# First loads of the attention stage and of the chain issued from ScalarE's queue, in a hybrid attention and RWKV-7 layer

## Chip, cores and metric

The kernel runs on one core of a Trainium2 chip. The metric is the device time of one execution in microseconds. The profile is of one execution of its own.

## What is computed

One layer over 2048 latent tokens of width 1024, arranged as a grid of 32 rows by 64 columns, with a prefix of 256 context tokens. A modulated input goes through one projection. Its columns feed eight heads of neighbourhood attention and eight RWKV-7 heads that run over the tokens in both directions. Both results go through an output projection, a layer norm and a squared-ReLU MLP.

```
p = modulate(x, sh1, sc1) @ w_in ; pc = modulate(xc, sh1c, sc1c) @ w_in
y_na = neighbourhood_attention(q, k, v, kc, vc, na_rpb)   # 8 x 16 window and all 256 context keys
...
S = S * w_t - s_kk (kk_t * a_t) + v_t k_t ; y_t = S r_t    # RWKV-7, two directions, from a state made by the context
...
x = layer_norm(ALPHA * x + g1 * concat(y_na, y_rw) @ w_out)
x = layer_norm(ALPHA * x + g2 * squared_relu_mlp(modulate(x, sh2, sc2)))
```

## The kernel before

The program has four stages. The first projects all tokens and writes queries, keys, values and the RWKV terms to scratch tensors in DRAM (`Q`, `KR` rotated keys, `KC` context keys, `VN` values, `AR`, `BK`, `VT`, `XB` for the chain). The second, `tail`, runs the attention and the RWKV chain side by side until about 1790 us; then come the output tiles with the rest of the chain, and two stages of the MLP.

The attention works on four pairs of heads. For a pair, 32 tiles of 128 queries are handled in groups of four. `front` makes scores of one tile against the window (`psl`, from the keys `kr` and the queries `qz`) and against the context (`psx`, from `kc`), takes the softmax on VectorE and ScalarE; `back`, three tiles later, transposes and multiplies with the values `vw` and `vc`. All products are made from a high and a low part of each operand: a load brings the 32-bit value, ScalarE casts the high part, VectorE (later GpSimd) subtracts it for the low part.

The chain goes in 36 steps of 64 tokens, both directions per step. `chain_pre` loads a step's `bkc`, `ks`, `SV` and `xz` and makes its first products; `chain_main` does the state update. In `tail` the two are woven: the first tile of the attention, then `chain_pre` for step 0, the second tile, then each step with the tiles that fall to it. The values of the first pair, `vload(0, 0, 8)`, are put after the chain's first `xz` load.

The order on each engine is not the order of the code alone: the framework schedules the instructions, and each engine and each DMA queue then runs its own in order. All loads before the change go through SyncE's queue (`nc.sync`). A DMA is issued by an engine as an instruction, which first waits for its semaphores. There are eight completion semaphores, `DMAHW0` to `DMAHW7`, handed out in turn over the DMAs of both queues; a DMA waits until the DMA that had the same semaphore before it has landed.

The names and lines of the opening, in the numbering of the kernel before: `kload` L916 and L917, L918 (keys of the first pair in two parts of 768 and 1280 columns), `pair` L937 (`bu`), L943 and L944 (`kc` and its cast), L947 (`vc`), `queries` L958, L960 and L961 (`qz`, casts, low parts; four DMAs of 64 KB per group), `vload` L925 (16 DMAs of 128 KB), `chain_pre` L1118 (`bkc`), L1125 (`ks`), L1128 (`SV`, four DMAs of 64 KB), L1130 (`xz`), the stores of rotated keys of the stage before, L717 (`KR<-rot`), and the last projected rows, L453.

Of the kernel before, what the change touches and what calls it, by code (L numbers as in the profile page):

```python
# [17 lines left out]
L = 256  # L18
# [10 lines left out]
CW = (0, 8, 24, 32)  # L29
# [28 lines left out]
def f32(ap):  # L58
    return ap.bitcast(F32)


class Kern:
# [858 lines left out]
    def vload(self, p, b0, b1):  # L921
        v = self.VN[L:, p * 128:(p + 1) * 128].rearrange("(b r x) c -> r x b c", r=4, x=64)
        for c in range(4):
            for r in range(4):
                self.nc.sync.dma_start(self.vw[r * 32:r * 32 + 32, b0:b1, c, :], v[r, CW[c]:CW[c] + 32, b0:b1, :])  # L925

    def attention(self):

        nc, a = self.nc, self.a
# [4 lines left out]
        def pair(p):  # L934
            E = nc.gpsimd if p else nc.vector
            u = self.at2.tile([128, 3, 12, 32], F32, name="bu")
            nc.sync.dma_start(u, a["rpb"][p])  # L937
            m = self.at2.tile([128, 3, 12, 32], F32, name="bm")
            for k in range(3):
                E.tensor_tensor(u[:, k], u[:, k], self.cmask[:, k, None, :].to_broadcast([128, 12, 32]), ALU.add)  # L940
                E.tensor_tensor(m[:, k], u[:, k], self.rmask[:, :, None].to_broadcast([128, 12, 32]), ALU.add)
            kc = [self.at2.tile([128, L], F32R, name="kc%d" % j) for j in range(2)]
            nc.sync.dma_start(f32(kc[1]), self.KC[p])  # L943
            nc.scalar.copy(kc[0], f32(kc[1]))  # L944
            E.tensor_tensor(kc[1], f32(kc[1]), f32(kc[0]), ALU.subtract)
            vc = self.at2.tile([128, 2, 128], F32, name="vc")
            nc.sync.dma_start(vc, self.VN[0:L, p * 128:(p + 1) * 128].rearrange("(m q) c -> q m c", q=128))  # L947
            return u, m, kc, vc

        def queries(g):  # L950

            p, hf, c, _ = tiles[g * 4]
            z = self.qz[g % 2]
            h, l = z
            for d in range(2):
                hs = slice(d * 64, d * 64 + 64)
                for j in range(2):
                    nc.sync.dma_start(f32(l[hs, j, :, hs]), self.Q[p, hs, j].rearrange("k (a c x) -> k c a x", c=4, x=64)[:, c, hf * 4:hf * 4 + 4, :])  # L958
            for j in range(2):
                nc.scalar.copy(h[:, j], f32(l[:, j]))  # L960
                (nc.gpsimd if g > 1 else nc.vector).tensor_tensor(l[:, j], f32(l[:, j]), f32(h[:, j]), ALU.subtract)  # L961

        def blocks(q):

            return {0: (1, 3), 7: (0, 2)}.get(q, (0, 3))

        def front(n):
            p, hf, c, i = tiles[n]
            q = hf * 4 + i
            if n == 0:  # L970
                self.kload(0, 0, 12)
                self.kload(0, 12, 32)
                st["pair", 0] = pair(0)
            if n == 0:
                queries(0)
            if i == 0 and n < 124:
                queries(n // 4 + 1)
            u, bm, kc, vc = st["pair", p]
            qh, ql = self.qz[n // 4 % 2]
            k0, k1 = blocks(q)  # L980
            w = (k1 - k0) * 128
            psl = self.psA.tile([128, 512], F32, name="psl")
            r = 4 * (q - 1 + k0)
            kh, kl = [x[:, r:r + 4 * (k1 - k0), CW[c]:CW[c] + 32] for x in self.kr]
            for j, (x, y) in enumerate(((qh, kh), (ql, kh), (qh, kl))):
                nc.tensor.matmul(psl[:, :w], lhsT=x[:, 0, i, :], rhs=y, start=j == 0, stop=j == 2)
            psc = self.psA.tile([128, 256], F32, name="psx")
            for j, (x, y) in enumerate(((qh, kc[0]), (ql, kc[0]), (qh, kc[1]))):
                nc.tensor.matmul(psc, lhsT=x[:, 1, i, :], rhs=y, start=j == 0, stop=j == 2)
            S = self.at2.tile([128, 640], F32, name="S", bufs=4)  # L990
            m = self.at2.tile([128, 8], F32, name="mx", bufs=4)

            lo, co = (k0 * 128, 384) if hf == 0 else (256, 0)
            sl, sc = S[:, lo:lo + w], S[:, co:co + 256]
            bias = (bm if k1 - k0 == 3 else u)[:, CK[c], 4 if q == 0 else 0:8 if q == 7 else 12, :]
            nc.vector.tensor_tensor_reduce(sl, psl[:, :w], bias.rearrange("p a b -> p (a b)"), 1.0, -3.0e38, ALU.add, ALU.max, m[:, 0:1])
            nc.vector.tensor_reduce(m[:, 1:2], psc, AX.X, ALU.max)
            nc.vector.tensor_scalar(m[:, 2:3], m[:, 0:1], m[:, 1:2], -1.0, ALU.max, ALU.mult)
            nc.scalar.activation(sc, psc, AF.Exp, bias=m[:, 2:3], accum_out=m[:, 4:5])
            nc.scalar.activation(sl, sl, AF.Exp, bias=m[:, 2:3], accum_out=m[:, 3:4])  # L1000
            nc.vector.tensor_tensor(m[:, 5:6], m[:, 3:4], m[:, 4:5], ALU.add)
            nc.vector.reciprocal(m[:, 6:7], m[:, 5:6])
            x = S[:, min(lo, co):min(lo, co) + w + 256]
            nc.gpsimd.tensor_scalar(x, x, m[:, 6:7], 1.0, ALU.mult, ALU.mult)
            st["S", n] = S, min(lo, co), w + 256
            if i == 3 and c == 3 and p < 3:
                if hf == 0:
                    self.kload(p + 1, 0, 12)
                else:
                    self.kload(p + 1, 12, 32)  # L1010
                    st["pair", p + 1] = pair(p + 1)
# [66 lines left out]
        for n in range(ASTEPS):  # L1078
            if n < 128:
                front(n)  # L1080
            if 0 <= n - LAG < 128:
                back(n - LAG)
            if n - LAG >= 128:
                for f in pieces[:5]:
                    f()
                del pieces[:5]
            if n == 1:
                with self.tc.issue_after(self.xzd):
                    self.vload(0, 0, 8)
            yield  # L1090
# [9 lines left out]
    def chain_pre(self, s, order):  # L1100

        nc = self.nc
        c = [order[d][s] for d in range(2)]
        last = s == 35
        T2 = lambda n, sh: self.ch2.tile(sh, F32, name=n)
        hs = [slice(0, 64), slice(64, 128)]
# [3 lines left out]
        sv = T2("SV", [128, 2, 4, 2, 64])  # L1110
# [14 lines left out]
                    nc.sync.dma_start(ks[h][hs[h], d, :, 0:w], self.AR[hs[h], d, c[d], :, 0:w])  # L1125
        for h in range(2):
            for d in range(2):
                nc.sync.dma_start(sv[hs[1 - h], d, :, h, :],  # L1128
                                  self.VT[c[d] * 64:(c[d] + 1) * 64, :].rearrange("t (p h v) -> t p h v", p=4, h=2)[:, :, h, :])
        self.xzd = nc.sync.dma_start(xz, self.XB.rearrange("s d (c p) t -> s (d c) p t", p=4)[:, two]).ins  # L1130
        ab = T2("ab", [128, 2, 4, 64])
# [802 lines left out]
```

## Time and profile before

| | us |
|---|---|
| median of 3 runs | 3431.05 (3422.89 to 3433.24) |
| profiled execution, its time | 3430.26 |
| its span, first to last instruction | 3428.5 |
| TensorE busy | 3193.7 (93%) |
| VectorE busy | 2603.2 (76%) |
| ScalarE busy | 1523.1 (44%) |
| GpSimd busy | 511.6 (15%) |
| last product of the projections | 1002.4 |
| first product of the attention | 1017.2 |
| last scores of the attention | 1731 |

The span is cut into stretches by the starts of the instructions. SyncE's and ScalarE's DMA instructions are in the timeline of these engines, with the time that the issue took; the transfer comes after it. A wait is put down to the instruction that came last.

### The profile page before, as it was taken

The numbers are of one execution on the slowest core, as the hardware profiler recorded it, in microseconds if no ns is written. First come the engines' busy times: TensorE is split into PE (matmuls) and PEld (weight loads), VectorE is DVE, ScalarE is ACT, GpSimd is POOL, SyncE is SP. The second block draws the span as 40 slices with busy tenths as digits, with TensorE's granted clock in tenths as the row PEclk, the third lists the DMA queues.
The fourth block names the chain that finished last, engine by engine and source line by source line (L and its number), as shares of the span: only waits on it lengthen the run. The fifth ranks groups of instructions, "written<-read, shape, count | busy, mean of one in ns | idle before, by whom it ended". The sixth has DMA issues, their size and how long they took to land. (4 is left out here: it accounts for less than half of the span.)

```text
span 3428.5 us, 65249 instructions
## 1 busy us (share of the span) xinstructions
PE 3193.7 (93%) x25176; PEld 2605.3 (76%) x25176; DVE 2603.2 (76%) x4907; ACT 1523.1 (44%) x2891; POOL 511.6 (15%) x535
## 2 busy tenths in 40 slices
PE   7999899899978999989879988999999989999998
PEld 3888888789866777767657766777788868888886
DVE  5567977888687778767768877767767657899878
ACT  4555465456535445454442123343433343337333
POOL 0000000000005454544343322000000000010001
PEclk9999999999989999999989988999999999999999
DMA  7487376726666655554374546665644455545441
GB/s 242 134 246 209 95 178 161 223 76 168 169 191 156 140 133 129 138 131 117 98 202 147 172 155 217 213 205 186 215 155 137 154 193 162 167 153 210 148 155 73
DMA packets 765338, 561.67 MB, mean 164 GB/s; under 512 B 380412, under 2 KB 653564, under 8 KB 763620
## 3 DMA queue, kind: packets, MB, share of 16 engines
q1 hardware_dynamic: 691738, 523.14, 51.8%
q10 hardware_dynamic: 73290, 34.37, 3.5%
q8 instruction: 198, 3.24, 0.4%
q14 instruction: 112, 0.92, 0.1%
HBM read 359.70 MB, written 197.66 MB: 163 GB/s over the span
## 5 line engine op out<-in xcount | busy, mean ns | idle before, releaser
L450 PE MATMUL psm<-xh,wh 128*128 128x386 f32 (+1 forms) x1104 | 381.7, 348 | 16.5 <-ACT row L453 9.9
L450 PE MATMUL psm<-xl,wh 128*128 128x386 f32 (+1 forms) x1104 | 381.4, 346 | 2.7 <-DVE xl L421 2.6
L450 PE MATMUL psm<-xh,wl 128*128 128x386 f32 (+1 forms) x1104 | 377.0, 341 | 0.0
L450 PEld LDWEIGHTS psm<-xh,wh 128*128 128x128 f32 x1104 | 210.9, 192 | 42.7 <-ACT row L453 18.7
L450 PEld LDWEIGHTS psm<-xl,wh 128*128 128x128 f32 x1104 | 210.7, 191 | 17.8 <-issue 7.3
L450 PEld LDWEIGHTS psm<-xh,wl 128*128 128x128 f32 x1104 | 210.6, 191 | 4.9 <-issue 3.7
L1531 PE MATMUL psa<-xh,w1h 128*128 128x512 f32 x512 | 204.3, 399 | 4.0 <-DVE p L1557 3.7
L1795 POOL TENSOR_TENSOR acc<-acc,g 128x1024 f32<-128x1024 f32 x8 | 28.9, 3641 | 1186.9 <-DVE acc L1738 1186.9
L1531 PE MATMUL psa<-xl,w1h 128*128 128x512 f32 x512 | 202.7, 396 | 0.0
L1531 PE MATMUL psa<-xh,w1l 128*128 128x512 f32 x512 | 201.8, 395 | 0.0
L1679 ACT CAST ah<-al 128x1024 fp32r<-128x1024 f32 x98 | 103.0, 1051 | 216.5 <-DMA al<-HU 204.8
L760 DVE TENSOR_TENSOR stmp<-mp,xp 128x1 f32<-128x1 f32 (+30 forms) x310 | 179.2, 578 | 18.3 <-POOL xp L752 6.8
L1680 DVE TENSOR_TENSOR al<-al,ah 128x1024 fp32r<-128x1024 f32 x98 | 121.3, 1237 | 86.8 <-ACT ah L1679 86.7
L436 DVE TENSOR_TENSOR wl<-wst,wh 128x1024 fp32r<-128x1024 f32 x81 | 98.7, 1219 | 92.0 <-ACT wh L435 69.6
L1462 ACT CAST w1h<-w1s 128x512 fp32r<-128x512 f32 x96 | 59.6, 621 | 238.3 <-DVE w1s L1451 84.5
L1729 PE MATMUL psqb<-uh,ah 128*128 128x512 f32 x384 | 149.6, 392 | 9.1 <-ACT uh L1635 9.1
L1729 PE MATMUL psqa<-uh,ah 128*128 128x512 f32 x400 | 154.8, 391 | 3.2 <-ACT uh L1635 3.2
L1729 PE MATMUL psqa<-ul,ah 128*128 128x512 f32 x400 | 157.3, 393 | 0.3 <-DVE ul L1635 0.3
L1729 PE MATMUL psqa<-uh,al 128*128 128x512 f32 x400 | 157.0, 392 | 0.0
L761 DVE TENSOR_REDUCE xp<-stmp 128x1 f32<-128x1 f32 (+30 forms) x310 | 153.9, 496 | 3.3
L1729 PE MATMUL psqb<-ul,ah 128*128 128x512 f32 x384 | 150.5, 392 | 0.0
L1729 PE MATMUL psqb<-uh,al 128*128 128x512 f32 x384 | 150.3, 391 | 0.0
(393 smaller groups left out, 8818.4 us busy)
## 6 DMA issues: line engine op xcount, KB each, us to landing
al<-HU SPq DMA_DIRECT2D x106, 512.0 KB, 3.6
wst<-in_w_in SPq DMA_DIRECT2D x81, 512.0 KB, 4.3
w<-in_mlp_w SPq DMA_DIRECT2D x32, 1024.0 KB, 7.7
wp<-in_mlp_w SPq DMA_DIRECT2D x32, 1024.0 KB, 6.4
wmod<-in_w_mod SPq DMA_DIRECT2D x48, 512.0 KB, 5.3
HU<-p SPq DMA_DIRECT2D x96, 256.0 KB, 3.9
HU<-s SPq DMA_DIRECT2D x84, 256.0 KB, 2.0
bkc<-BK SPq DMA_DIRECT2D x36, 512.0 KB, 4.8
```

The lines of the kernel that those rows point to most:

```text
L436: nc.vector.tensor_tensor(wl, w, f32(wh), ALU.subtract)
L450: nc.tensor.matmul(ps[:, :y - x], lhsT=s[:, k, :], rhs=m[:, k, x:y], start=(i == 0), stop=(i == 23))
L760: nc.vector.tensor_tensor(tv, mp[:, i:i + 1, lo:lo + n].to_broadcast([128, n, n]), xp[:, lo:lo + n, lo:lo + n], ALU.mult)
L761: nc.vector.tensor_reduce(xp[:, lo:lo + n, i], tv, AX.X, ALU.add)
L1462: made[n] = nc.scalar.copy(h, x).ins, V.tensor_tensor(l, x, f32(h), ALU.subtract).ins
L1531: nc.tensor.matmul(ps, lhsT=w[:, k, :], rhs=x[:, k, :], start=(i == 0 and pr in (1, 5, 2)), stop=(i == 11), skip_group_check=True)
L1679: fs += [lambda: nc.scalar.copy(ah, f32(al)), fb[0], lambda: V.tensor_tensor(al, f32(al), f32(ah), ALU.subtract), fb[1]]
L1680: lambda: V.tensor_tensor(al, f32(al), f32(ah), ALU.subtract), fb[1]]
L1729: nc.tensor.matmul(ps, lhsT=x[:, c, s], rhs=y[:, c, :], start=(i == 0 and new), stop=(i == 5 and end), skip_group_check=True)
L1795: (V if 4 * i + j in VMUL else G).tensor_tensor(row, row, g2, ALU.mult)
```

## The change

The loads of the first pair are issued from ScalarE's queue in place of SyncE's: the four loads of the first group of queries, `kc` and `vc` of pair 0, the four `SV` loads of chain step 0, and, of the sixteen `vw` loads of pair 0, the four of column block 0. In the code the first queries also come ahead of the keys.

```diff
@@ vload @@
-                self.nc.sync.dma_start(self.vw[r * 32:r * 32 + 32, b0:b1, c, :], v[r, CW[c]:CW[c] + 32, b0:b1, :])
+                (self.nc.sync if p or c else self.nc.scalar).dma_start(self.vw[r * 32:r * 32 + 32, b0:b1, c, :], v[r, CW[c]:CW[c] + 32, b0:b1, :])
@@ attention, pair @@
-            nc.sync.dma_start(f32(kc[1]), self.KC[p])
+            (nc.sync if p else nc.scalar).dma_start(f32(kc[1]), self.KC[p])
...
-            nc.sync.dma_start(vc, self.VN[0:L, p * 128:(p + 1) * 128].rearrange("(m q) c -> q m c", q=128))
+            (nc.sync if p else nc.scalar).dma_start(vc, self.VN[0:L, p * 128:(p + 1) * 128].rearrange("(m q) c -> q m c", q=128))
@@ attention, queries @@
-                    nc.sync.dma_start(f32(l[hs, j, :, hs]), self.Q[p, hs, j].rearrange("k (a c x) -> k c a x", c=4, x=64)[:, c, hf * 4:hf * 4 + 4, :])
+                    (nc.sync if g else nc.scalar).dma_start(f32(l[hs, j, :, hs]), self.Q[p, hs, j].rearrange("k (a c x) -> k c a x", c=4, x=64)[:, c, hf * 4:hf * 4 + 4, :])
@@ attention, front @@
             if n == 0:
+                queries(0)
                 self.kload(0, 0, 12)
                 self.kload(0, 12, 32)
                 st["pair", 0] = pair(0)
-            if n == 0:
-                queries(0)
@@ chain_pre @@
-                nc.sync.dma_start(sv[hs[1 - h], d, :, h, :],
+                (nc.sync if s else nc.scalar).dma_start(sv[hs[1 - h], d, :, h, :],
```

Since the framework schedules, the order moves with it. SyncE's queue at the opening, first before, from the first keys on (`qz_10871` is the first group of queries, `qz_10874` the second; in brackets what the DMA waits for):

```order
L916 DMA kr_10877<-KR 128x768 [waits DMAHW7_49]
L916 DMA kr_10877<-KR 128x1280 [waits DMAHW0_49]
L937 DMA bu<-in_rpb 128x1152 [waits DMAHW1_49]
L943 DMA kc_10899<-KC 128x256 [waits DMAHW2_49,Activation_49]
L717 DMA KR<-rot 128x384 [waits DMAHW3_49,DVE_49]
L947 DMA vc<-VN 128x2x128 [waits DMAHW4_49]
L958 DMA qz_10871<-Q 64x4x64 [waits DMAHW5_49,Pool_49]
```

And with the change:

```order
L916 DMA kr_10877<-KR 128x768 [waits DMAHW2_49]
L717 DMA KR<-rot 128x384 [waits DMAHW4_49,DVE_49]
L916 DMA kr_10877<-KR 128x1280 [waits DMAHW6_49]
L937 DMA bu<-in_rpb 128x1152 [waits DMAHW0_49]
L1095 DMA tm<-in_tri 128x256 [waits DMAHW3_49,DMAHW2_49]
L958 DMA qz_10874<-Q 64x4x64 [waits DMAHW4_49,Pool_49]
L958 DMA qz_10874<-Q 64x4x64 [waits DMAHW6_49]
L958 DMA qz_10874<-Q 64x4x64 [waits DMAHW0_49]
L958 DMA qz_10874<-Q 64x4x64 [waits DMAHW2_49]
L1117 DMA bkc<-BK 128x2x512 [waits DMAHW4_49]
```

The first queries, `kc` and `vc` are gone from SyncE; the second part of the keys now stands behind a store of rotated keys, and the semaphores go in steps of two. After the chain's first `xz` twelve `vw` loads follow where there were sixteen, then the second step's `bkc`.

ScalarE's queue at the opening, before:

```order
L453 COPY row<-psm 128x386 [waits PE_49]
L917 CAST kr_10876<-kr_10877 128x768 [waits DMAHW7_49]
L917 CAST kr_10876<-kr_10877 128x1280 [waits DMAHW0_49]
L944 CAST kc_10898<-kc_10899 128x256 [waits DMAHW2_49]
L960 CAST qz_10870<-qz_10871 128x512 [waits DMAHW7_49,DMAHW5_49,Pool_49]
```

And with the change, after two `vw` loads and the four loads of the first queries that follow the copy of the last row:

```order
L917 CAST kr_10876<-kr_10877 128x768 [waits DMAHW2_49]
L943 DMA kc_10907<-KC 128x256 [waits DMAHW1_49]
L960 CAST qz_10870<-qz_10871 128x512 [waits DMAHW5_49]
L947 DMA vc<-VN 128x2x128 [waits DMAHW3_49]
L1127 DMA SV<-VT 64x4x64 [waits DMAHW6_49,DMAHW4_49,DMAHW0_49]
L960 CAST qz_10870<-qz_10871 128x512 [waits DMAHW7_49]
L917 CAST kr_10876<-kr_10877 128x1280 [waits DMAHW6_49]
L1127 DMA SV<-VT 64x4x64
L1127 DMA SV<-VT 64x4x64 [waits DMAHW1_49]
L944 CAST kc_10906<-kc_10907 128x256
L1127 DMA SV<-VT 64x4x64 [waits DMAHW3_49]
L925 DMA vw<-VN 32x8x128 [waits DMAHW5_49]
```

The casts of the queries move ahead of the second cast of keys, the cast of `kc` behind it and behind three `SV` loads.

## Rows read from the trace of the kernel before

**Rows 1.** Busy time by stretch: stretch, length, busy us of each engine, clock, DMA, GB/s.

```profile
1002.73:1017.19 14.46, 0.00 (x1) 0.01 (x1) 8.27 (x17) 3.65 (x6) 2.73 (x3) 0.58 0.84 243
...
1045.00:1732.00 687.00, 626.36 (x9306) 491.76 (x9305) 528.88 (x1527) 339.58 (x919) 337.55 (x378) 0.96 0.53 129
```

**Rows 2.** TensorE's waits, 1002 to 1045 us: us in total, times, longest.

```profile
PE psl L986 <- ACT qz L960: 14.5, 1, 14.5
PE psg L1141 <- DMA ks<-AR: 4.5, 1, 4.5
PE psl L986 <- DVE qz L961: 3.7, 1, 3.7
```

**Rows 3.** SyncE's timeline: start us, duration us, line, operation, tiles, count.

```profile
1006.26 0.92 SPq L916 DMA_DIRECT2D kr<-KR  x2
...
1007.75 0.38 SPq L943 DMA_DIRECT2D kc<-KC  x1
1008.22 0.60 SPq L717 DMA_DIRECT2D KR<-rot  x1
1008.87 0.46 SPq L947 DMA_DIRECT2D vc<-VN  x1
1009.43 5.85 SPq L958 DMA_DIRECT2D qz<-Q  x6
...
1017.24 0.60 SPq L1118 DMA_DIRECT2D bkc<-BK  x1
...
1020.48 2.58 SPq L1128 DMA_DIRECT2D SV<-VT  x4
1023.10 0.60 SPq L1130 DMA_DIRECT2D xz<-XB  x1
1023.75 9.47 SPq L925 DMA_DIRECT2D vw<-VN  x16
1033.53 0.38 SPq L1118 DMA_DIRECT2D bkc<-BK  x1
```

**Rows 4.** TensorE's timeline before the second chain step, idle time before in brackets.

```profile
1036.02 0.69 PE L1194 MATMUL us<-SV,btc 128*64 128x64 f32 x16
1041.21 0.45 PE L1141 MATMUL psg<-ks,bkc 64*64 64x64 f32 x2 [4.51 <-DMA ks<-AR]
```

**Rows 5.** ScalarE's timeline at the opening.

```profile
1010.03 0.83 ACT L917 CAST kr<-kr 128x768 fp32r<-128x768 f32 x1 [6.78 <-DMA kr<-KR]
1012.50 1.26 ACT L917 CAST kr<-kr 128x1280 fp32r<-128x1280 f32 x1 [1.65 <-DMA kr<-KR]
1014.34 0.41 ACT L944 CAST kc<-kc 128x256 fp32r<-128x256 f32 x1 [0.58 <-DMA kc<-KC]
1016.51 1.14 ACT L960 CAST qz<-qz 128x512 fp32r<-128x512 f32 x2 [1.77 <-DMA qz<-Q]
```

**Rows 6.** DMA issues, 1000 to 1045 us: count, size, median us from issue to landing.

```profile
ks<-AR SPq DMA_DIRECT2D x12, 64.0 KB, 4.8
...
qz<-Q SPq DMA_DIRECT2D x8, 64.0 KB, 2.5
```

**Rows 7.** VectorE's timeline: the low parts of both groups of queries.

```profile
1020.78 2.91 DVE L961 TENSOR_TENSOR qz<-qz,qz 128x512 fp32r<-128x512 f32 x4
```

**Rows 8.** Busy time by stretch, as rows 1, for DMA share and clock.

```profile
1004.00:1008.00 4.00, 0.00 (x0) 0.00 (x0) 3.11 (x7) 0.00 (x0) 1.51 (x2) 0.62 0.52 156
1008.00:1016.00 8.00, 0.00 (x0) 0.00 (x0) 3.23 (x5) 2.49 (x3) 0.00 (x0) 0.50 1.00 285
1016.00:1028.00 12.00, 7.15 (x46) 5.39 (x46) 10.07 (x22) 3.94 (x9) 3.92 (x5) 0.50 0.72 183
1028.00:1040.00 12.00, 8.70 (x91) 7.29 (x91) 5.63 (x19) 6.03 (x18) 3.73 (x5) 0.78 1.21 208
...
1041.20:1045.00 3.80, 3.79 (x40) 3.27 (x40) 1.07 (x5) 0.59 (x1) 0.00 (x0) 0.50 0.64 192
```

**Rows 9.** TensorE's longest wait in total, 1045 to 1790 us.

```profile
PE psg L1141 <- DMA ks<-AR: 19.2, 18, 3.3
```

## The prediction

> **What bounds the kernel now.** The page comes first: TensorE is busy for 93% of the span, so time can only be gained where it stands idle. The table by stretch shows where that is near the change [rows 1]: in the 14.46 us after the last projection TensorE does nothing, DMA runs at a share of 0.84 and 243 GB/s, and the granted clock goes down to the lower of its two levels, 1.2 GHz of 2.4. In the 687 us of the attention stage after 1045 TensorE is busy for 626.36 us; little is to be had there. The waits of TensorE between 1002 and 1045 us then give three idle pieces with their last releaser [rows 2]: 14.5 us until ScalarE has cast the first queries, 3.7 us until VectorE has made their low parts, 4.5 us until the second chain step's `ks` has landed. Together 22.7 us; this is all the change can reach directly.
>
> SyncE's timeline says why the loads are late [rows 3]. From 1006.26 to 1033.53 us SyncE does nothing but issue, one load after another. The first queries wait behind the keys, `bu`, `kc` and `vc`: six take 5.85 us from 1009.43. The second step's `bkc` stands behind all sixteen `vw` loads, 9.47 us from 1023.75, and is issued only at 1033.53. TensorE is through with its work at 1036.71 and goes on at 1041.21 [rows 4]. ScalarE in the same time is free: it waits 6.78 us for the first keys and casts at 1010.03, 1012.50, 1014.34 and 1016.51, with gaps between [rows 5].
>
> **What is moved, part by part.** Fourteen DMAs of the first pair go from SyncE's queue to ScalarE's; none is added. Their issue time on SyncE, by the rows: four `qz` at 5.85/6, 3.90 us; `kc` 0.38; `vc` 0.46; four `SV` 2.58; four `vw` at 9.47/16, 2.37. Sum 9.69 us [rows 3]. That would bring the second `bkc` from 1033.53 to 1023.84 if SyncE only issued.
>
> It does not only issue. The new order shows that while both queues are active SyncE's DMAs carry the even semaphores and ScalarE's the odd ones, so SyncE waits for its own DMA of four before, not eight. I follow it. `tm` waits for the first keys, which land at 1010.03 [rows 5]. The 1280-column keys now stand behind a `KR` store that waits for VectorE until 1008.22; they are issued at 1008.82 in place of 1006.7 [rows 3], so they land 0.5 to 2.1 us later than the 1012.50 at which ScalarE got them [rows 5]. The second load of the next queries waits for them, the third for `bu`, the fourth for `tm`; each lands some 2.5 us after issue [rows 6]. The first `bkc` comes to about 1016.0 instead of 1017.24, `ks` to 1016.6; its third load and `xz` wait for `SV` loads that ScalarE issues only between casts, so that `xz` goes out near 1019.8 instead of 1023.10. Twelve `vw` take 12 x 0.59 = 7.1 us and wait about 1.3 us for the last `vw` of ScalarE. The second `bkc` is issued at 1019.8 + 0.6 + 7.1 + 1.3 = 1028.8 or a little before: I take 5.2 us gained, between 2 (the waits stretch) and 9.69 (no wait).
>
> On ScalarE the fourteen issues cost 0.4 to 0.6 us each, 8 us, most of them in its idle time. Two `vw` loads stand first there, ahead of the queries, and two queries wait for them to land; that is hidden, since the first keys are not there before 1010.03. The first TensorE product then needs the cast of these keys (to 1010.86), the issue of `kc` (0.38) and a cast of queries (1.14/2): 1011.8 instead of 1017.19. But ScalarE also has `SV` loads between its casts, some of which wait for a landing, and the cast of `kc` goes from 1014.34 to about 1016.5. VectorE ends its preparation with the low parts of the next queries, 2.91 us for all four from 1020.78 before [rows 7]; they wait for the same four-deep queue and end near 1022.7 instead of 1023.69. So of the 5.4 us at the first product I keep 2 us by the time TensorE stands before the second step: 1034.7 in place of 1036.71. The bounds are -3 (the later cast of `kc` sets the pace) and 10.0 (all of the 6.3 us between the first keys' cast and 1017.19, with the 3.7 us behind it).
>
> There the second step's `ks` decides. It landed at 1041.21 and lands 5.2 us earlier, at 1036.0; landing times of 4.8 us are usual here [rows 6]. TensorE is there at 1034.7 and waits 1.3 us, where it waited 4.5: it goes on 5.2 us earlier. The 4.5 us had a second cost [rows 8]: the granted clock fell, and in the 3.80 us after the idle piece TensorE worked at 0.50, the 1.2 GHz level. At the full clock that work takes half, 1.9 us less. A shorter idle piece may or may not keep the clock; I take 0.9, between 0 and 1.9. The last three `SV`, `xz` and so on of this step move with it and are not counted again.
>
> After 1045 I cost the change at nothing. The work is the same, the order of the instructions is not: it differs here and there up to the output tiles. The waits in question are those for `ks`, 19.2 us in 18 pieces [rows 9]. Counted in the two orders, the closest of these loads of whole steps is held back until 17 TensorE instructions before its user in both, and the median is 43 before and 41 now, so I expect as many and as long waits.
>
> The sum: 5.2 + 0.9 = 6.1 us off the profiled execution's 3430.26 us gives **3424.2, say 3424 us**. That execution is 0.8 us under the median of the runs, 3431.05.
>
> One row speaks against the whole: between 1008 and 1016 us the DMA share is 1.00 at 285 GB/s, and 1.21 between 1028 and 1040 [rows 8]; there another queue can only change the turn of the transfers. The Trainium skill, "DMA: Bandwidth & Descriptors", section "Issuing engines are not separate DMA queues", says just that: DMAs of all issuing engines run on the same 16 DMA engines, and a second issuing engine only saves the issue time. By it alone the gain is at most the issue time, 9.69 us, and the sum 3420.6, and it is nothing wherever the engines are full; the trace agrees for these two stretches. But at 1004 to 1008 the share is 0.52 and at 1016 to 1028 0.72 [rows 8]: the queries and two `vw` (512 KB) can now run in the first gap. So the row leaves room for my 5.2 us and hardly for 9.69.
>
> **Rivals.** *The transfers bound the opening.* The first keys and `bu` take as long as before, ScalarE's loads share the engines with them, the four-deep waits take back the issue time, and TensorE goes on at 1041 as before. For it: the share of 1.00 and 1.21; against it: the gaps. Time 3430.
>
> *The opening closes up.* The first product comes at 1012, the low parts and `kc` are no bound, `ks` is there when asked for: 5.4 + 3.7 + 4.5 + 1.9 = 15.5 us off, 3415. For it: ScalarE is idle where its new loads stand; against it: the casts behind waiting `SV` issues.
>
> *The new order costs more later.* The place is TensorE's first product of each chain step; the load of `ks` is held until an earlier step has freed its buffer. If the new order leaves each of the 18 waits a microsecond longer, that is 18 us, against 6 gained: 3442. It decides when the lead of these loads gets shorter than their landing time by more than it is. The order speaks against it, the 19.2 us that are there [rows 9] for it.
>
> **The numbers.** A measurement of this kernel can tell about 0.3%, 10.3 us, from no change. Forecast 0.44, transfers bound 0.26, opening closes up 0.22, later cost 0.08. Under 3420.8 lies nearly all of the third case and a fifth of the first: 0.28 faster. Over 3441.4 most of the last: 0.07 slower. The rest, 0.65, is the same. Range 3412 to 3436: the bounds of the sum reach from 3433 (-3) to about 3414, and three runs of the kernel lay 10 us apart.
>
> **What would show it.** Right: first product near 1012, second step's `bkc` issued at 1028 to 1029, `ks` waits of TensorE before it under 2 us, no half clock at 1041 to 1045, attention's end some 6 us earlier. Wrong: `bkc` after 1032, SyncE waiting long for its own loads, a cast of `kc` after 1018 with TensorE waiting for it, or more than 25 us of waits for `ks` after 1045.

## The result and the profile after

The change made the kernel slower: median 3445.22 us of five runs (3443.29 to 3457.76) against 3430.02 us of five, ratio 1.0054, 95% interval 1.0038 to 1.0069. The forecast was 3424, its range 3412 to 3436, and a time over 3441.4 had been given a chance of 0.07. Ratios and intervals, here and below, are those on record over all runs of both kernels; the quotient of the two medians can differ a little (here it is 1.0044).

| us | before | after |
|---|---|---|
| profiled execution, its time | 3430.26 | 3444.7 |
| its span | 3428.5 | 3442.5 |
| TensorE busy | 3193.7 | 3209.6 |
| VectorE, ScalarE, GpSimd busy | 2603.2, 1523.1, 511.6 | 2608.9, 1525.8, 506.8 |
| start of the last projection product | 1002.4 | 996.3 |
| from there to the attention's first product | 14.8 | 11.4 |
| to the second chain step's first product | 38.8 | 36.0 |
| to the first output product (L1346, L1345 after) | 789.6 | 800.5 |
| to the first product of the MLP (L1531, L1530 after) | 1107.7 | 1125.9 |
| to the end of the span | 2426.1 | 2446.3 |

The projections have the same order in both kernels, and in all profiled executions of this study they end somewhere between 994.8 and 1002.4 us; so times are counted from there. Lines from L975 on are one lower with the change.

The opening, to be read beside [rows 2 to 5]. TensorE's waits from 996 to 1039 us (us in total, times, longest):

```profile
PE psl L985 <- ACT qz L960: 11.0, 1, 11.0
PE psg L1140 <- DMA ks<-AR: 5.3, 2, 4.4
PE psx L988 <- ACT kc L944: 4.0, 1, 4.0
```

ScalarE's timeline:

```profile
1005.33 0.37 ACTq L943 DMA_DIRECT2D kc<-KC  x1
...
1006.97 0.62 ACT L960 CAST qz<-qz 128x512 fp32r<-128x512 f32 x1 [0.82 <-DMA qz<-Q]
...
1010.02 1.25 ACT L917 CAST kr<-kr 128x1280 fp32r<-128x1280 f32 x1
1012.19 0.52 ACTq L1127 DMA_DIRECT2D SV<-VT  x1
1012.75 0.40 ACT L944 CAST kc<-kc 128x256 fp32r<-128x256 f32 x1 [1.48 <-DMA kc<-KC]
```

SyncE's timeline:

```profile
1006.17 6.40 SPq L958 DMA_DIRECT2D qz<-Q  x4
1012.79 0.43 SPq L1117 DMA_DIRECT2D bkc<-BK  x1
...
1017.29 0.38 SPq L1129 DMA_DIRECT2D xz<-XB  x1
1017.72 6.06 SPq L925 DMA_DIRECT2D vw<-VN  x12
1024.11 0.38 SPq L1117 DMA_DIRECT2D bkc<-BK  x1
```

TensorE's timeline before the second step, and the stretch behind it (length, busy us and count of TensorE, its weight loads, VectorE, ScalarE, GpSimd, clock, DMA share, GB/s):

```profile
1032.29 0.44 PE L1140 MATMUL psg<-ks,bkc 64*64 64x64 f32 x2 [4.37 <-DMA ks<-AR]
```

```profile
1032.20:1036.00 3.80, 3.71 (x22) 2.73 (x24) 0.30 (x2) 0.86 (x2) 0.00 (x0) 0.50 0.62 199
```

One wait of 14.5 us became one of 11.0, but a new one of 4.0 for the cast of `kc` stands behind it, and the wait for the second step's `ks` is 4.37 us where it was 4.51 [rows 4], again with the lower level of the clock, 1.2 GHz, behind it. The opening is worth 2.8 us at that point: the second step's first product comes 36.0 us after the last projection, from 38.8.

Behind the opening, 2.8 us ahead become 18.2 us behind at the MLP. The waits for `ks`, the place that the prediction had watched [rows 9], are not longer (TensorE's waits, 1039 to 1790 us):

```profile
PE psg L1140 <- DMA ks<-AR: 16.0, 18, 2.9
PE psx L988 <- ACT S L998: 9.7, 11, 1.6
PE ry L1172 <- DVE yacc L1207: 8.5, 4, 5.6
```

What changed is told by two stretches: from the second step's first product to the first output product (the attention stage), and on to the MLP's first product (the output stage). Before:

```profile
1041.21:1792.01 750.80, 673.77 (x10121) 527.71 (x10121) 567.37 (x1588) 362.66 (x962) 360.62 (x397) 0.95 0.55 137
1792.01:2110.06 318.05, 297.99 (x2410) 222.29 (x2409) 251.58 (x475) 79.93 (x187) 96.14 (x81) 0.94 0.51 163
```

After:

```profile
1032.29:1796.80 764.51, 691.54 (x10129) 536.49 (x10129) 576.37 (x1596) 368.67 (x969) 363.05 (x402) 0.93 0.55 136
1796.80:2122.15 325.35, 299.86 (x2421) 223.76 (x2420) 250.34 (x468) 78.90 (x186) 92.01 (x80) 0.93 0.50 157
```

Length less busy time is idle time: in the attention stage 77.0 us before and 73.0 after. TensorE did not wait more. It was busy 17.8 us longer with the same products, at a granted clock of 0.93 in place of 0.95. In the output stage idle time grew from 20.1 to 25.5 us.

### The profile page after: what moved, and what is told of

It is laid out like the page before. It is cut to its first block, busy times and chain, and to the rows that moved or that the text cites. A ratio compares the mean times of both kernels' runs of the same rounds, so it can differ in the third digit from the quotient of the medians.

```text
span 3442.5 us, 65246 instructions
## 1 busy us (share of the span) xinstructions
PE 3209.6 (93%) x25176; PEld 2611.6 (76%) x25176; DVE 2608.9 (76%) x4907; ACT 1525.8 (44%) x2891; POOL 506.8 (15%) x535
## 4 chain that ended last, share of the span: by engine, by line
PE 46%; DVE 14%; DMA 8%; issue 3%; ACT 2%; SPq 1%; POOL 1%; ACTq 0%; DVEq 0%; POOLq 0%
PE psa L1530 9%; PE psqb L1728 7%; PE psqa L1728 7%; PE psb L1530 4%; PE ops L1345 3%; PE pse L1530 2%; DMA ks<-AR 2%; PE psv L1050 2%; DVE stmp L760 1%; PE psg L1140 1%; PE psl L985 1%; PE pst L1021 1%; DVE ks L1147 1%; PE psx L988 1%; DVE xp L761 1%
## 5 line engine op out<-in xcount | busy, mean ns | idle before, releaser
L1530 PE MATMUL psa<-xh,w1h 128*128 128x512 f32 x512 | 204.7, 400 | 7.7 <-DVE p L1556 4.0
L1530 PE MATMUL psa<-xl,w1h 128*128 128x512 f32 x512 | 203.4, 397 | 0.0
L1530 PE MATMUL psa<-xh,w1l 128*128 128x512 f32 x512 | 202.3, 396 | 0.0
```

Of the source, the lines that this page charges most:

```text
L1530: nc.tensor.matmul(ps, lhsT=w[:, k, :], rhs=x[:, k, :], start=(i == 0 and pr in (1, 5, 2)), stop=(i == 11), skip_group_check=True)
```

## The experiments

The framework had ordered every engine anew, from the opening to the last output tile: of the 7464 places between the first and the last difference on TensorE, 6485 hold another instruction. To part the order from the queue, the kernels below (names in e, b and r) carry a table of instructions per engine, and each instruction is tied to the one that the table names before it. A table does hold the order: in `b3_step2` below, whose table is that of the kernel before save for five loads on SyncE, VectorE's 4907 instructions follow each other in the trace as in that of the kernel before. No run has a table and nothing else; that the ties cost nothing to speak of is seen in `e1_open`, which has them and is as fast as before.

```diff
     k.phase1()
     k.tail()
+    pin_order(tc)   # add_manual_dep(ins, last.name, no semaphore) along the table, engine by engine
```

### Opening or rest

`e1_open` has the change's code; its table is the order of the change up to the second chain step's first product, then that of the kernel before.

> The changed opening (fourteen loads from ScalarE's queue, the new order of all engines up to the second chain step's first product), and from there on, on every engine, the order of the kernel before. Theory (the new order of the rest costs): the opening's gain of some 3 us stays and the loss goes, 3424 to 3429 us, ratio to before 0.998 to 1.000. Rival (the loads on ScalarE's queue cost, by late casts and waits of four loads back, and push everything behind them): 3441 to 3447 us, as slow as the change, ratio 1.0035 to 1.005.

Measured: 3436.22 us against 3434.5, ratio 1.0001 (0.9992 to 1.0011). The 3 us that were expected to stay, a ratio of 0.9992, lie at the edge of the interval; this run can't tell them from nothing.

`e2_rest` is the mirror: every `nc.scalar` of the change back to `nc.sync` (the table, not the place of the code, decides the order), the order of before first, that of the change from the second step on.

> The mirror of the run above: all loads on SyncE's queue and the order of the kernel before up to the second chain step's first product, then the order of the changed kernel on every engine. Theory (the new order of the rest costs): 3444 to 3450 us, ratio to before 1.004 to 1.006, slower than the change itself by the lost 3 us or equal to it. Rival (the queue costs): 3428 to 3433 us, ratio 0.9995 to 1.001.

Measured: 3451.23 us, ratio 1.0062 (1.0040 to 1.0084). The intervals lie apart. With no load on ScalarE and the old opening the kernel is as slow as the change; with the changed opening and the old rest it is as fast as before. The loss is the new order behind the opening, and the changed opening by itself is worth nothing that can be measured.

`e3_tail` and `e4_tailb` put the border at the first output product.

> The order of the kernel before, all loads on SyncE, up to the first output tile's product; from there on the order of the changed kernel. Theory (both stretches of the new order cost by themselves, some 10 us in the attention stage and some 8 in the output stage): 3436 to 3440 us, ratio 1.002 to 1.003. If the loss in the output stage is only a consequence of the attention stage before it: 3429 to 3432 us. Rival (the queue costs): 3429 to 3432 us as well.

> The changed kernel up to the first output tile's product; from there on the order of the kernel before. Theory (both stretches cost by themselves): 3435 to 3439 us, ratio 1.0015 to 1.0025. If the output stage's loss is a consequence of the stage before it, or if the queue costs: 3443 to 3447 us.

Measured: `e3_tail` (old order, then the change's output stage) 3448.19 us, 1.0045 (1.0030 to 1.0061); `e4_tailb` (the change's order, then the old output stage) 3445.04 us, 1.0032 (1.0018 to 1.0046). Each half of the new order costs by itself. `e3_tail` lost more than expected (1.002 to 1.003), and the middle of `e4_tailb` lies above what was expected too (1.0015 to 1.0025). The intervals of the two overlap, so which half costs more stays open. The stretches of `e3_tail`:

```profile
1038.97:1796.25 757.28, 680.33 (x10125) 532.18 (x10125) 566.43 (x1592) 362.70 (x962) 363.06 (x398) 0.94 0.56 136
1796.25:2124.28 328.03, 300.93 (x2405) 224.63 (x2404) 251.53 (x471) 80.01 (x187) 92.28 (x81) 0.92 0.51 157
```

And of `e4_tailb`:

```profile
1030.85:1805.87 775.02, 697.50 (x10144) 541.38 (x10145) 573.89 (x1596) 367.01 (x967) 363.12 (x402) 0.93 0.54 134
1805.87:2121.18 315.31, 294.23 (x2407) 219.99 (x2405) 247.19 (x468) 78.85 (x187) 92.94 (x79) 0.95 0.52 163
```

The lengths go with the order of the stage, not with what came ahead of it.

### A new order without a new queue

`m1_move` keeps all loads on SyncE and only moves the code of the first queries; the framework orders the rest as it will.

```diff
             if n == 0:
+                queries(0)
                 self.kload(0, 0, 12)
                 self.kload(0, 12, 32)
                 st["pair", 0] = pair(0)
-            if n == 0:
-                queries(0)
```

> No load changes its queue: all are on SyncE as before. Only the code of the first queries stands ahead of the keys, as in the change, and the framework orders everything anew (two thirds as many instructions of TensorE stand elsewhere as in the change). Theory (what costs is that the stage after the opening got another order, whatever the edit was): slower than before, 3437 to 3450 us, ratio 1.001 to 1.0055. Rival (the cost comes with the loads on ScalarE's queue): 3429 to 3434 us, ratio 0.999 to 1.001.

Measured: 3450.05 us against 3436.2, ratio 1.0040 (1.0026 to 1.0054). No load changed its queue, and there is a loss of nearly the size of the change's. It is not the same loss, as its attention and output stages show:

```profile
1034.45:1814.06 779.61, 687.02 (x10106) 539.12 (x10106) 569.23 (x1588) 363.69 (x963) 358.77 (x397) 0.93 0.55 133
1814.06:2129.08 315.02, 295.62 (x2421) 221.62 (x2421) 250.29 (x470) 79.04 (x187) 90.89 (x80) 0.95 0.52 163
```

Here TensorE is idle for 92.6 us of the attention stage, where the kernel before has 77.0 and the change 73.0, and the output stage is no longer than before. An order can cost by waits as well as by busy time.

`m3_sv` and `m2_qkv` are parts of the change in the code of before, also ordered by the framework.

```diff
-                nc.sync.dma_start(sv[hs[1 - h], d, :, h, :],
+                (nc.sync if s else nc.scalar).dma_start(sv[hs[1 - h], d, :, h, :],
```

> The kernel before with one part of the change alone, the four SV loads of the first chain step on ScalarE's queue (1.7 to 2.6 us of issue), ordered anew by the framework. By the opening alone it would be 3428 to 3434 us. Theory (any new order of the rest is worth several us, of either sign, but the one before was a good one): 3436 to 3450 us, ratio 1.001 to 1.0055. Rival (the loads of queries, kc, vc and vw are what costs): 3428 to 3434 us.

Measured: 3436.9 us, 1.0002 (0.9990 to 1.0014), a miss for the theory: this new order costs nothing.

```diff
-            nc.sync.dma_start(f32(kc[1]), self.KC[p])
+            (nc.sync if p else nc.scalar).dma_start(f32(kc[1]), self.KC[p])
...
-                    nc.sync.dma_start(f32(l[hs, j, :, hs]), self.Q[p, hs, j]...
+                    (nc.sync if g else nc.scalar).dma_start(f32(l[hs, j, :, hs]), self.Q[p, hs, j]...
```

(`vc` likewise.)

> The kernel before with the first queries, kc and vc alone on ScalarE's queue, ordered anew by the framework. Theory (any new order): 3433 to 3450 us; the first product comes 3 to 4 us earlier relative to the last projection, and this does not show in the time. Rival (the early queries are worth what they save): 3424 to 3429 us, ratio 0.998 to 0.9995.

Measured: 3440.47 us, 1.0027 (1.0007 to 1.0047). The expectation of an earlier first product was wrong: it came 15.1 us after the last projection. In this order two of the four query loads stand on ScalarE's queue behind the cast that waits for the first keys, and went out only 9.2 us after the last projection. Four orders that the framework made from small edits lie between 1.0002 and 1.0054 of the one before, none under it.

### What the attention stage loses

The profiled executions of all kernels with a table give a sample for each order of the attention stage. Idle time is length less busy time; the last column is TensorE's busy time within the spells of the lower clock, summed over the trace's clock records.

| attention stage, mean us (smallest to largest) | length | idle | busy | busy at 1.2 GHz |
|---|---|---|---|---|
| order of before, 7 kernels (before, e1, e3, b1 twice, b2, b3) | 755.3 (750.8 to 762.2) | 76.7 | 678.6 | 74.1 (62.5 to 86.6) |
| order of the change, 8 (after, e2, e4, r1 to r5) | 771.7 (764.5 to 782.1) | 78.1 | 693.6 | 99.6 (88.5 to 122.6) |

The lengths don't overlap. Of 16.4 us idle time is 1.4. If work at half the clock takes twice as long, the 25.5 us more at 1.2 GHz cost 12.8. The traces give a little less: within either order, a trace with one more us at 1.2 GHz has 0.42 to 0.44 us more of busy time (the slope of a line through its 7 or 8 traces), so an estimate from them is 11. The other 2 to 4 us are busy time that the clock does not explain. The loss of this stage is mostly clock: there is as much idle time as before, and more of the work is done at the lower level. This is an account of the traces; no run held the clock up by itself. That the places of the idle pieces decide it is likely but not shown, and which rows of the order bring the clock down is open.

### What the output stage loses

Here the two orders differ in one thing that can be pointed at. A chain step has groups of products (L1172, then L1183 and L1187, then L1201 and L1193) that wait for another engine's work on the group ahead. In both orders products of the output tiles (L1345) stand between these groups, 18 to 42 per step, save in the first step or two and the last two. In the change one step in the middle has none; its 25 stand ahead of it. TensorE's order with the change (in these lists a small f32 product counts once; the trace has two records for it):

```order
8226 L1345 MATMUL ops<-wol,yh 128x512
...
8234 L1172 MATMUL ry<-SV,ks_22370 64x64
8235 L1183 MATMUL ry<-ks_22369,SV 64x64
...
8242 L1183 MATMUL ry<-ks_22370,SV 64x64
8243 L1187 MATMUL us<-rh_22905,xz_10882 64x64 x8
8244 L1201 MATMUL ry<-ab,SV 64x64
8245 L1193 MATMUL us<-SV,btc 64x64 x8
8246 L1201 MATMUL ry<-ab,SV 64x64 x7
8247 L1140 MATMUL psg<-ks_23052,bkc 64x128
```

TensorE's timeline there, with idle time in brackets:

```profile
1911.66 0.69 PE L1183 MATMUL ry<-ks,SV 128*64 128x64 f32 x16 [1.37 <-ACT rh L1174]
1914.50 0.33 PE L1201 MATMUL ry<-ab,SV 64*64 64x64 f32 x2 [1.55 <-ACT SV L1188]
1915.75 0.79 PE L1193 MATMUL us<-SV,btc 128*64 128x64 f32 x16 [0.93 <-DVE SV L1189]
1919.60 0.44 PE L1140 MATMUL psg<-ks,bkc 64*64 64x128 f32 x1 [2.01 <-DMA ks<-AR]
```

And the stretch around it:

```profile
1905.00:1936.00 31.00, 24.51 (x252) 18.09 (x251) 20.38 (x37) 6.46 (x17) 7.46 (x7) 0.83 0.66 191
```

The output stage took 325.4, 328.5 and 328.0 us in the three kernels that have the change's order there unedited (after, e2, e3), and 315.3 to 322.0 in the seven that have that of before; the m kernels, whose orders leave no such step, took 315.0 to 318.2. Here idle time counts too: the mean of the three is 8.8 us over that of the seven, 4.7 of it idle time and 4.0 busy time, with 38.8 us of work at 1.2 GHz in place of 31.0. `r1_cover` is the change with its own table and this edit on TensorE (and what other engines do with these products moved behind their work for the step):

```diff
-L1345 x25, L1172 x8, L1183 x8, L1187 x8, L1201, L1193 x8, L1201 x7, L1140
+L1345 x9, L1172 x8, L1345 x8, L1183 x8, L1187 x8, L1345 x8, L1201, L1193 x8, L1201 x7, L1140
```

> The changed kernel, its own order kept, with one edit in the output stage: of the 25 output products in a row ahead of the chain step that has none between its parts, eight are put behind that step's first part and eight behind its third, and what VectorE, ScalarE and GpSimd do for these products goes behind their work for the step. Theory (this uncovered step is what the output stage lost: waits for rh, SV, SV and ks of 6.4 us and 10.2 us at the lower clock in place of 3.4): the stage from the first output product to the first product of the MLP takes 317 to 321 us in place of 325 to 328, the time is 4 to 8 us less than that of the change, ratio to before 1.003 to 1.0045. Rival (the products moved leave their own place uncovered, or the next tile comes late): stage 324 to 329 us, ratio 1.005 to 1.006.

Measured: 3456.77 us against 3435.0, ratio 1.0059 (1.0043 to 1.0076), stage 329.2 us, as the rival had it. The wait for `rh` fell to 0.59 us and those for `SV` went, but the next wait grew (TensorE, then SyncE):

```profile
1919.09 0.69 PE L1183 MATMUL ry<-ks,SV 128*64 128x64 f32 x16 [0.59 <-ACT rh L1174]
1930.55 0.44 PE L1140 MATMUL psg<-ks,bkc 64*64 64x128 f32 x1 [6.63 <-DMA ks<-AR]
```

```profile
1920.27 0.39 SPq L1332 DMA_DIRECT2D xres<-in_x  x1
1925.79 0.37 SPq L1330 DMA_DIRECT2D yt<-YN  x1
1926.26 1.28 SPq L1121 DMA_DIRECT2D ks<-AR  x2
```

The `ks` load stands behind that of `yt`, which waits for VectorE's work on the tile ahead, and that I had put later. `r2_both` (with the cover) and `r3_ks` (without) were to move `ks` ahead of the tile's stores.

```diff
-L1364 X, L1367 XN, L1332 xres, L1330 yt, L1121 ks x2
+L1121 ks x2, L1364 X, L1367 XN, L1332 xres, L1330 yt
```

> r1_cover with the next step's two ks loads issued ahead of the stores and loads of the output tile behind which they stood on SyncE. In r1_cover that ks came 6.6 us late, since it is queued behind a load of yt that waits for work which was put later. Theory (the uncovered step and the ks behind yt together are what the output stage lost): no wait over 1 us for ks at this place, stage from the first output product to the MLP's first 316 to 321 us in place of 325 to 329, ratio to before 1.003 to 1.0045. Rival (the tile that comes later costs elsewhere, the stage's loss is spread): stage 323 to 328 us, ratio 1.005 to 1.0065.

> The changed kernel with only these two ks loads moved ahead on SyncE; the step stays without output products between its parts. If the waits for ks (2.6 us) and the lower clock behind them decide: stage 320 to 323 us, ratio 1.004 to 1.005. If the uncovered parts decide (waits for rh, SV and SV of 3.8 us stay): stage 323 to 327 us, ratio 1.005 to 1.006, as the change.

Measured: 3466.05 us, 1.0087 (1.0067 to 1.0106), and 3462.75 us, 1.0084 (1.0066 to 1.0101), against 3432.26. Both edits hit another pair than meant, that of an earlier step, so they don't answer the question. They show something else: with two loads moved ahead by four places of a queue the output stage took 335.1 us in `r3_ks`, 7 to 10 more than in the three kernels with the change's order unedited, and there is a new wait 101 us into the stage:

```profile
1900.45 1.19 PE L1172 MATMUL ry<-SV,ks 128*64 128x64 f32 x16 [5.14 <-DVE yacc L1207]
```

`r4_ksyt` and `r5_cover3` move the right pair; the second also spreads the cover.

```diff
-L1330 yt, L1121 ks x2
+L1121 ks x2, L1330 yt
 (r5_cover3, TensorE)
-L1345 x9, L1172, L1345 x8, L1183, L1187, L1345 x8, L1201, L1193, L1201
+L1345 x5, L1172, L1345 x6, L1183, L1187, L1345 x6, L1201, L1193, L1201, L1345 x8
```

> r1_cover with the two ks loads that were late there issued just ahead of the yt load (r2_both and r3_ks had moved the pair of the step before, which then held the tile's stores). These loads replace the ks that the uncovered step itself still reads, so they can go out only after that step's third group of products. Theory (uncovered step and late ks together are the output stage's loss): the wait for ks falls from 6.6 to 1 to 3 us, stage 320 to 325 us, ratio 1.0035 to 1.005. Rival (the loss is spread, or moves on): stage 325 to 330 us, ratio 1.005 to 1.006.

> As r4_ksyt, with the output products spread as 5, 6, 6 and 8: the last eight stand behind the step's last part, ahead of the products that wait for ks. Theory: wait for ks under 1.5 us, a wait of 1 to 2.5 us for yacc ahead of the step's first part, stage 318 to 323 us, ratio 1.003 to 1.0045. Rival (the loss is spread, or moves on): stage 325 to 330 us, ratio 1.005 to 1.006.

Measured: 3455.18 us, 1.0054 (1.0034 to 1.0073), stage 326.4 us; 3457.31 us, 1.0060 (1.0040 to 1.0079), stage 328.6 us, against 3436.38. Both theories missed. At the uncovered step itself most was mended: in `r5_cover3` the waits for `ks` there are 0.96 and 0.28 us (2.4 us for `yacc` and 1.1 for `rh` are left), and the clock around it is 0.95 where it was 0.83:

```profile
1920.00:1953.00 33.00, 25.01 (x278) 18.22 (x274) 21.59 (x38) 7.35 (x19) 8.46 (x8) 0.95 0.57 184
```

Ten us on, the tile that was delayed holds TensorE in its turn:

```profile
1945.94 0.63 PE L1153 MATMUL psg<-ident,bkc 128*128 128x128 f32 x4 [3.29 <-DVE frs L210]
```

So the uncovered step is a place where the order of the change loses time in the trace, but covering it gave the stage nothing back: other waits came in its place. That the output stage's order costs is shown (e3 and e4); that this one step is the reason is not.

### The opening with the old order kept

`b1_best` keeps the order of before from the second step on, and puts the opening in another order:

```diff
 SyncE
-kr x2, bu, kc, KR, vc, qz x4, (next) qz x2, tm, qz x2, bkc, ks x4, SV x4, xz, vw x16, bkc, ks x4, SV x4, xz
+kr x2, bu, KR, bkc, ks x4, tm, (next) qz x4, SV x4, xz, bkc, ks x4, xz, SV x4, vw x16
 ScalarE
-kr cast, kr cast, kc cast, qz cast x2
+qz x4, kc, vc, kr cast, qz cast, kc cast, qz cast, kr cast
```

(VectorE's low parts of `qz` and `kc` go ahead of the second part of the keys.)

> The order of the kernel before is kept on every engine from the second chain step on. In the opening the first queries, kc and vc are issued by ScalarE right after its last copy, ahead of its casts, the casts and low parts of the queries come ahead of the second part of the keys, the chain's first loads come ahead of the next queries, and the second step's loads ahead of the sixteen vw loads. Theory (the opening is worth what it saves if the rest keeps its order): first product 10 to 11 us after the last projection in place of 14.5, no wait for the second step's ks, that step's first product 30 to 33 us after the last projection in place of 38.8, time 3422 to 3430 us, ratio 0.997 to 0.999. Rival (time gained in the opening is given back in the attention stage, which another wait sets): 3431 to 3437 us, ratio 0.9995 to 1.001.

> The kernel of the run b1_best once more, since its gain of 0.25% is near what can be told. If the gain is real: ratio 0.996 to 0.999. If it was chance: 0.9995 to 1.001.

Measured: 3427.79 us against 3436.2, ratio 0.9975 (0.9961 to 0.9988), and again 3425.43 us against 3435.0, 0.9979 (0.9960 to 0.9998). It is faster than both kernels. The first product came 11.1 us after the last projection, just above the 10 to 11 expected; the second step's 35.1, where 30 to 33 was expected; and there was no wait for its `ks`. Up to there the trace gains 3.7 us on the kernel before; the medians gain 8 to 10, and where the rest comes from is not shown.

`b2_sync` has the same order with all loads on SyncE.

```diff
-rmask, KR, kr x2, bu, ... vw x16
+rmask, qz x4, KR, kr x2, kc, bu, ... vc, vw x16
```

> The order of b1_best on every engine, but with all loads on SyncE's queue: the first queries ahead of the last store of rotated keys, kc behind the keys, vc behind the chain's loads. No second queue is left. Theory (the order of the loads is what helps, the second queue is not): 3424 to 3431 us, ratio 0.9965 to 0.9988. Rival (the issue time on SyncE matters, so the second queue is needed): first keys 2 to 3 us later, 3431 to 3437 us, ratio 0.999 to 1.001.

Measured: 3430.02 us, 0.9990 (0.9977 to 1.0003). The first product came 11.1 us after the last projection here too, and the second step's 34.0: no second queue was needed for that. The Trainium skill, "DMA: Bandwidth & Descriptors", section "Issuing engines are not separate DMA queues", says that issuing from several engines saves only the time of the issue; the opening of this run agrees. By the time it lies between `b1_best` and before and is told from neither: 0.9990 is at the edge of what the rival had (0.999 to 1.001) and outside the theory's ratios, so whether the second queue is worth something in the time stays open.

`b3_step2` is the kernel before with five loads moved on SyncE.

```diff
-xz, vw x16, bkc, ks x4
+xz, bkc, ks x4, vw x16
```

> The kernel before, its order kept on every engine, with one edit: the second chain step's bkc and ks (five loads) are issued ahead of the sixteen vw loads. Theory: the wait of 4.5 us for ks and the lower clock behind it go, the first product stays at 14.5 us after the last projection; 4 to 6 us off, 3429 to 3433 us where before is 3435, ratio 0.998 to 0.9995. Rival (the next loads are what TensorE then waits for, or the attention stage gives it back): ratio 0.9995 to 1.001.

Measured: 3428.29 us, 0.9985 (0.9973 to 0.9996), as expected. SyncE's timeline, then TensorE's:

```profile
1019.57 0.47 SPq L1117 DMA_DIRECT2D bkc<-BK  x1
1020.09 2.57 SPq L1124 DMA_DIRECT2D ks<-AR  x4
1022.70 9.05 SPq L925 DMA_DIRECT2D vw<-VN  x16
```

```profile
1029.73 0.33 PE L1140 MATMUL psg<-ks,bkc 64*64 64x64 f32 x2
...
1036.79 0.33 PE L1172 MATMUL ry<-SV,ks 128*64 128x64 f32 x2 [2.04 <-DMA SV<-VT]
1037.93 0.34 PE L1172 MATMUL ry<-SV,ks 128*64 128x64 f32 x4 [0.81 <-DMA SV<-VT]
```

The second step's first product comes 31.5 us after the last projection in place of 38.8, earlier than with fourteen loads on another queue; of the wait for `ks` nothing is left, and 2.8 us of wait for `SV` take its place, so that some 20 us later the lead of 7.3 us is down to 4.6.

## Why the prediction was wrong

**What failed: "After 1045 I cost the change at nothing."** That step looked at one wait, for `ks`, found its lead unchanged in both orders and took the rest for equal, on the ground that the order differs "here and there". On the `ks` waits it was right: 16.0 us against 19.2 [rows 9]. But the order of the attention and output stages had changed at most places, and `e2_rest` puts the price of that at 0.62% (0.40 to 0.84), in place of nothing. By the traces the attention stage took 16.4 us more in the mean, the output stage 8.8. The idle time of a wait was also the wrong thing to count: in the attention stage it hardly grew, while busy time did, most of it by the clock. The prediction priced the clock only at the one idle piece of 4.5 us.

**The rival "the new order costs more later"** gave 3442 us for an execution that took 3444.7, with a chance of 0.08. Its size was right by luck, for its place was wrong: not eighteen waits for `ks`, but the clock in the attention stage, and an output stage longer by 7 us in the two traces.

**The opening, forecast at 6.1 us, gave 2.8** in the trace (5.2 were forecast up to the second step's first product, 0.9 by the clock behind it), and nothing that can be measured in `e1_open`. Step by step, from the last projection:

- The first product was put at 9.4 us and came at 11.4, from 14.8. The direction was right.
- SyncE's waits for its own load of four before were foreseen, but too short: the four next queries took 6.40 us. The 5.85 us for six before [rows 3] were read as issue alone, but 1.8 of them are waits too, for the keys and `bu`. `xz`, put at 17.4, went out at 21.0, no earlier than the 20.7 before. Only the twelve `vw` in place of sixteen brought the second `bkc` forward, from 31.1 to 27.8, where 26.4 was forecast.
- The cast of `kc` came at 16.5 in place of 14.1, from 11.9 before [rows 5]. Its load stood on ScalarE's queue behind the cast that waits for the first keys, went out some 9 us after the last projection (5.4 before) and was there 6.8 us later (6.6 before). TensorE waited 4.0 us for the cast, which had been named as a sign of being wrong. It did not set the pace all the same: TensorE was through before the second step at 31.6, from 34.3, so 2.7 us earlier where 2 were forecast.
- The term that was mis-sized is the 5.2 us of `ks`: it was there at 36.0, where 33.6 was forecast. The wait for it was to fall to 1.3 us and stayed at 4.37; the gain by the clock was to be 0.9 and was none, since the stretch behind it is at 0.50 again [rows 8].

**The rival "the transfers bound the opening"** is not what happened: in `b3_step2` and `b1_best` the same bytes came early enough, by their order in the queue. **The opening did not close up** either: `kc` and `ks` still held TensorE for 4.0 and 4.37 us.

## What to carry to other kernels

Where a framework orders the instructions, a small edit at one place can be an edit of the whole order, and the price of that can be many times what the edit itself gains or costs (here between nothing in `m3_sv` and 0.54%): pin the old order, make the edit inside it, and only then judge the edit. In a queue that runs in order, ask first what stands ahead of the late load; five loads put ahead of sixteen brought the second step's first product to 31.5 us, fourteen loads on a second queue to 36.0. And when a stage grows, compare idle and busy time of the same products before looking for a wait.

## What the runs showed of the hardware

- The same products with nearly the same idle time (76.7 and 78.1 us in the mean) can take longer: by order the attention stage had TensorE busy at 1.2 GHz for 62.5 to 86.6 us or for 88.5 to 122.6.
- Executions with one order differ as well: the attention stage in the order of before took 750.8 to 762.2 us, and the projections, the same in all kernels, ended between 994.8 and 1002.4. One trace against one trace can't tell 10 us here; the ratios above rest on 5 to 29 runs each.
